# SwiGLU's first product: block sums and lower parts of the weights moved from VectorE to accumulating DMAs

## The chip, the cores and the metric

The kernel runs on one core of a Trainium2 chip. The metric is the device time of one execution in microseconds (us). Engines are named as in the profile: PE is TensorE, PEld its weight load, DVE VectorE, ACT ScalarE, POOL GpSimd, SP the queue from which the DMAs are issued in the kernel before.

## The reference

One layer of a streaming encoder in float32, 1024 tokens by 1024 channels: RMSNorm, one wide input projection for three mixers (convolution, gated linear attention, differential attention), gates, an output projection with residual, and then the channel mixing, where the change is:

```python
h = rms_norm(x, norm_ffn_g[l])
gate, up = jnp.split(h @ w_ffn_in[l], 2, axis=-1)
x = x + (jax.nn.silu(gate) * up) @ w_ffn_out[l]
```

`w_ffn_in` has 2 x 2816 columns, so that `h @ w_ffn_in` is a product of 1024 tokens by 1024 channels by 5632 columns.

## The kernel before

Every float32 product is made of three products of 1-pass operands: an operand is split into an upper part (`wh`, a rounded copy that ACT writes) and a lower part (`wl`, the operand less `wh`, which DVE writes), by `hilo` (L110 to L112), and `mm3` (L114 to L117) issues upper x upper, upper x lower and lower x upper. The loads are issued from SP.

The first product of SwiGLU goes over 22 units (`NU`) of 256 output columns, gate and up in turn. A unit's weights are 1 MB, four blocks of 128 x 512 (`a11`, `a21`, `a12`, `a22`; two halves of K by two halves of the columns). Each unit is taken by Winograd's form of Strassen's algorithm, in seven block products p = 0 to 6 in place of eight. Products 0, 3 and 5 have a plain block as left operand (`a11`, `a12`, `a22`); products 1, 2, 4 and 6 have sums of blocks: s1 = a21 + a22, s2 = s1 - a11, s3 = a11 - a21, s4 = a12 - s2, made on DVE by `comb` (L949 to L951). The right operands are blocks of h and their sums (`B`), made once ahead of the units in `ffn_norm`. A product is 4 steps of K by 3 matmuls of 512 columns, 12 matmuls.

The list `order` (L969 to L975) says in which order the products (unit, p) are taken, and `makes` in which order their operands are made. In the loop over `order`, `make()` runs seven products ahead (`AHEAD`, L62): it has the operand's sum made, then `operand()` (L133 to L137) splits it into one of eight pairs of buffers (`wh`, `wl`). The raw weights go into two buffers of half a unit (`wr`), the sums into four (`s2` with tag "s2", tiles named s1 to s4). The results are evicted behind the products: `copy` (ACT, L1006), `finish` (DVE adds, ACT silu for a gate unit; for an up unit DVE multiplies and SP stores to `m_d`, L991 to L1004). Each engine runs its instructions in the order in which they stand in its program, and a DMA that waits on SP or POOL holds up those that stand behind it there. That order is made by a recording layer, which moves instructions a little against the code, and semaphores do the rest.

Of the kernel before, what the change touches and what calls it, by code (L numbers as in the profile page):

```python
# [42 lines left out]
def units():  # L43
    """Order in which the 256-column weight units are consumed."""
    out = []
    for h in range(NH):
        out += [("CV", 2 * h), ("A", h), ("V", h), ("CV", 2 * h + 1), ("OG", h)]
        if h < NH - 1:
            out += [("MG", h)]
    for j in range(ND // 2):  # L50
        out += [("DV", j), ("QK", 2 * j), ("MD", j), ("QK", 2 * j + 1)]
    out += [("MG", NH - 1)] + [("MC", u) for u in range(4)]
    out += [("PW", u) for u in range(4)]
    out += [("WO", u) for _ in range(2) for u in range(4)]
    for j in range(FT // 2):
        out += [("FG", j), ("FU", j)]
    out += [("FO", j) for j in range(FT // 2)]
    return out
# [9 lines left out]
def body(nc, tc, I, out):  # L68
# [40 lines left out]

    def hilo(hi, lo, src):  # L110
        act.copy(hi, src)  # L111
        vec.tensor_tensor(out=lo, in0=src, in1=f(hi), op=ALU.subtract)  # L112

# [5 lines left out]
    def rstd(dst, ss, n, width):  # L119
        """dst = (ss / n + eps) ** -0.5"""  # L120
        vec.tensor_scalar(out=dst, in0=ss, scalar1=1.0 / n, scalar2=EPS, op0=ALU.mult, op1=ALU.add)
        pool.tensor_tensor(out=dst, in0=dst, in1=mhalf[:, 0:width], op=ALU.pow)  # L122

    # ---- weights: stream of units, one ahead of its use, split in pieces behind the products
    ready = deque()
# [48 lines left out]

    # ---- work that runs behind the projections: generators, each yields after how many
    # parts of a projection (8 products) it goes on
    events, clock = [], {"now": 0, "seq": 0, "conv": 0.0}
# [36 lines left out]

    # ---- hidden state, transposed: [channel, token] in two exact parts
    def transposed(src, hh, hl, half, gcol):
# [135 lines left out]

    # ================= A. convolution
    csum = q4("csum")[:, 0:S]
# [213 lines left out]

    # ================= C. differential attention
    A = {}  # L570
# [174 lines left out]

    # ================= convolution: LayerNorm over channels, swish
    def conv_norm(cs):
# [113 lines left out]
    def ffn_norm(t):  # L861
        xt = x2.pop(t)
        sp.dma_start(x2_d[t], xt)
        xn = b4("xn")
        ssc, rc = sm[:, 16 + t:17 + t], sm[:, 24 + t:25 + t]
        act.activation(xn, xt, AF.Square, accum_out=ssc)
        rstd(rc, ssc, D, 1)
        vec.scalar_tensor_tensor(out=xn, in0=xt, scalar=rc, in1=ffg, op0=ALU.mult, op1=ALU.mult)
        yield 4 if t in PARTS[0] else 3 if t < 4 else 2
        tt = slice(t % 4 * P, (t % 4 + 1) * P)  # L870
        v4 = lambda a: a.rearrange("p (k c) -> p k c", k=4)
        v4f = lambda a: a.bitcast(F32)

        def put(name, src):
            hilo(B[name][0][:, :, tt], B[name][1][:, :, tt], v4(src))

        pts = []
        for g in range(2):
            pt = bank()
            for k in range(4):  # L880
                pe.transpose(pt[:, k * P:(k + 1) * P], xn[:, (4 * g + k) * P:(4 * g + k + 1) * P], ident)
            pts.append(pt)
        old = lambda name, p: f(B[name][p][:, :, tt])
        if t < 4:
            put("11", pts[0])
            yield 2 if t in PARTS[0] else 0
            put("21", pts[1])
            return
        u, v = b4("u"), b4("v")
        t1, t2_, r12, t3 = u[:, hs(0)], u[:, hs(1)], v[:, hs(0)], v[:, hs(1)]  # L890
        vec.tensor_tensor(out=v4(t1), in0=v4(pts[0]), in1=old("11", 0), op=ALU.subtract)
        vec.tensor_tensor(out=v4(t1), in0=v4(t1), in1=old("11", 1), op=ALU.subtract)
        act.copy(r12, pts[0])
        put("T1", t1)
        yield 2 if t in PARTS[0] else 0
        vec.tensor_tensor(out=t2_, in0=pts[1], in1=t1, op=ALU.subtract)
        put("T2", t2_)
        yield 2 if t in PARTS[0] else 0
        put("22", pts[1])
        vec.tensor_tensor(out=t3, in0=pts[1], in1=r12, op=ALU.subtract)  # L900
        put("T3", t3)
# [25 lines left out]
    for half in range(2):  # L927
# [3 lines left out]
        for u in range(4):  # L931
            run(out_proj(half, u))
    # ================= SwiGLU, first product
    NU = FT
# [6 lines left out]
    def lefts(n):  # L941
        if n == 1:
            a11, a21, a12, a22 = (raw1[:, i, :] for i in range(4))
        else:
            r0 = raw_half(first + n, 0)
            r1 = raw_half(first + n, 1)
            a11, a21, a12, a22 = r0[:, 0:HALF], r0[:, HALF:], r1[:, 0:HALF], r1[:, HALF:]

        def comb(name, a, b, op):  # L949
            o = s2(name)  # L950
            vec.tensor_tensor(out=o, in0=a, in1=b, op=op)  # L951
            return o

        s_ = {}
        p = None
        while True:
            p = yield operand(s_[p]) if p is not None else None
            if p in (0, 3, 5):
                s_[p] = {0: a11, 3: a12, 5: a22}[p]
            elif p == 1:  # L960
                s_[1] = comb("s1", a21, a22, ALU.add)
            elif p == 2:
                s_[2] = comb("s2", s_[1], a11, ALU.subtract)
            elif p == 4:
                s_[4] = comb("s3", a11, a21, ALU.subtract)
            else:
                s_[6] = comb("s4", a12, s_[2], ALU.subtract)

    order = [(0, 0), (0, 3), (1, 0), (1, 3), (0, 1), (1, 1), (0, 2), (1, 2), (0, 4), (1, 4), (0, 6), (1, 6), (0, 5)]  # L969
    for n in range(1, NU):  # L970
        if n + 1 < NU:
            order.append((n + 1, 0))
        order += [(n, 5), (n, 6)] if n > 1 else [(n, 5)]
        if n + 1 < NU:
            order += [(n + 1, p) for p in range(1, 5)]  # L975
    makes = list(order)
# [5 lines left out]
    def make():  # L982
        if nxt[0] < len(makes):
            n, p = makes[nxt[0]]
            nxt[0] += 1
            if n not in gens:
                gens[n] = lefts(n)
                next(gens[n])
            made[n, p] = gens[n].send(p)

    def finish(n, i, k, add=None, src=None):  # L991
        gate = n % 2 == 0
        key = (n // 2, i, k)
        if add is not None:
            t = (y2 if len(fbs) == 0 else m2 if gate else c2)("t")
            vec.tensor_tensor(out=t, in0=src, in1=add, op=ALU.add)
            src = t
# [7 lines left out]

    def copy(src):  # L1006
        c = (c2 if fbs else y2)("c")
        act.copy(c, src)
        return c
# [12 lines left out]

    # the second product's operands
    mids, x3 = {}, {}
# [23 lines left out]
    for at, (n, p) in enumerate(order):  # L1048
# [35 lines left out]
        if p == 0:  # L1084
            ch["p1"] = copy(o)
        elif p == 2:
            ch["u2"] = copy(o)
        elif p == 3:
# [4 lines left out]
        elif p == 5:  # L1093
            finish(n, 1, 0, None, o)
        elif p == 6:
            finish(n, 0, 1, ch["u2"], o)

    drain()
    fbs[0].release()

    # ================= SwiGLU, second product, residual, RMSNorm
    fc = tc.alloc_tile_pool(name="fc", bufs=1)
# [107 lines left out]
```

## Time and profile before

| | |
|---|---|
| median of two runs | 2171.72 us (2170.72 to 2172.71) |
| span of the profiled execution | 2171.2 us, 0.5 us below the median |
| PE busy | 2147.5 us, 99% |
| DVE busy | 1385.6 us, 64% |
| ACT busy | 859.0 us, 40% |
| POOL busy | 45.5 us, 2% |
| SwiGLU's first product | from about 1497 to 1919 us of the span |

The table is read with the span: a busy share near 100% over the whole execution says that there is little room beside that engine, but the share of DVE or of ACT is a mean over stages, and what one stage waits for is read in that stage. PE's granted clock is a share of 2.4 GHz; 0.50 would be the lower of its two levels, 1.2 GHz.

### The profile page before, as it was taken

The numbers are of one execution on the slowest core, as the hardware profiler recorded it, in microseconds if no ns is written. First come the engines' busy times: TensorE is split into PE (matmuls) and PEld (weight loads), VectorE is DVE, ScalarE is ACT, GpSimd is POOL, SyncE is SP. The second block draws the span as 40 slices with busy tenths as digits, with TensorE's granted clock in tenths as the row PEclk, the third lists the DMA queues.
The fourth block names the chain that finished last, engine by engine and source line by source line (L and its number), as shares of the span: only waits on it lengthen the run. The fifth ranks groups of instructions, "written<-read, shape, count | busy, mean of one in ns | idle before, by whom it ended". The sixth has DMA issues, their size and how long they took to land.

```text
span 2171.2 us, 27863 instructions
## 1 busy us (share of the span) xinstructions
PE 2147.5 (99%) x10988; PEld 1787.7 (82%) x10988; DVE 1385.6 (64%) x2088; ACT 859.0 (40%) x1729; POOL 45.5 (2%) x45
## 2 busy tenths in 40 slices
PE   8999999999999999999999999999999999999998
PEld 6988988889887878778777888898888888888886
DVE  5988798789755454454545356567755545576766
ACT  6342251342345455455545354234433333341212
POOL 0000000000000000000000000000000000000000
PEclk9999999999999999999999999999999999999999
DMA  4112112121121111110111265443322222282111
GB/s 159 39 59 68 59 41 77 49 74 55 48 78 30 49 44 40 35 59 25 59 35 53 71 241 165 131 140 122 107 89 78 92 73 81 85 292 97 59 39 78
DMA packets 65059, 177.65 MB, mean 82 GB/s; under 512 B 6720, under 2 KB 17600, under 8 KB 64928
## 3 DMA queue, kind: packets, MB, share of 16 engines
q1 hardware_dynamic: 64928, 175.88, 24.4%
q8 instruction: 86, 1.41, 0.3%
q14 instruction: 45, 0.37, 0.1%
HBM read 137.58 MB, written 38.27 MB: 81 GB/s over the span
## 4 chain that ended last, share of the span: by engine, by line
PE 95%; DVE 3%; DMA 1%; issue 0%; POOL 0%; ACT 0%; SPq 0%; DVEq 0%; POOLq 0%; ACTq 0%
PE pb L115 22%; PE pb L116 22%; PE pb L117 22%; PE sc L115 6%; PE sc L116 5%; PE sc L117 5%; PE sc L643 3%; PE pb L678 3%; PE sc L642 3%; PE pb L667 1%; POOL sm L122 0%; DVE wl L112 0%; DVE xn L1127 0%; PE pb L712 0%; PE pb L504 0%
## 5 line engine op out<-in xcount | busy, mean ns | idle before, releaser
L115 PE MATMUL pb<-h,wh 128*128 128x512 f32 x1152 | 462.8, 402 | 0.0
L117 PE MATMUL pb<-h,wl 128*128 128x512 f32 x1152 | 450.9, 391 | 0.0
L116 PE MATMUL pb<-h,wh 128*128 128x512 f32 x1152 | 450.6, 391 | 0.0
L111 ACT CAST wh<-wr 128x512 fp32r<-128x512 f32 x331 | 203.5, 622 | 394.4 <-DVE x L1119 122.1
L112 DVE TENSOR_TENSOR wl<-wr,wh 128x512 fp32r<-128x512 f32 x331 | 225.5, 688 | 165.3 <-ACT wh L111 163.4
L362 DVE SCALAR_TENSOR_TENSOR acc<-up,par,acc 128x1024 f32<-128x1024 f32 x240 | 307.1, 1280 | 2.7
L115 PEld LDWEIGHTS pb<-h,wh 128*128 128x128 f32 x1152 | 217.1, 188 | 48.3 <-issue 5.1
L117 PEld LDWEIGHTS pb<-h,wl 128*128 128x128 f32 x1152 | 216.6, 188 | 46.8
L116 PEld LDWEIGHTS pb<-h,wh 128*128 128x128 f32 x1152 | 217.0, 188 | 41.3 <-DVE h L228 0.9
L1119 DVE TENSOR_TENSOR x<-x,pb 128x512 f32<-128x512 f32 x176 | 120.0, 684 | 59.8 <-PE pb L117 59.2
L115 PE MATMUL pb<-wh,h 128*128 128x256 f32 x512 | 148.1, 289 | 0.0
L117 PE MATMUL pb<-wh,h 128*128 128x256 f32 x512 | 144.9, 283 | 0.0
L116 PE MATMUL pb<-wl,h 128*128 128x256 f32 x512 | 144.8, 283 | 0.0
L115 PE MATMUL sc<-bT,wh 128*128 128x512 f32 x352 | 137.0, 390 | 0.5 <-ACT bT L111 0.5
L116 PE MATMUL pb<-wl,mh 128*128 128x512 f32 x352 | 136.9, 389 | 0.0
L115 PE MATMUL pb<-wh,mh 128*128 128x512 f32 x352 | 136.9, 389 | 0.0
L117 PE MATMUL pb<-wh,ml 128*128 128x512 f32 x352 | 136.9, 389 | 0.0
L116 PE MATMUL sc<-bT,wh 128*128 128x512 f32 x352 | 136.8, 389 | 0.0
L117 PE MATMUL sc<-bT,wl 128*128 128x512 f32 x352 | 136.6, 389 | 0.0
L111 ACT CAST wh<-s 128x512 fp32r<-128x512 f32 x88 | 54.5, 621 | 129.5 <-PE sc L116 79.4
L115 PEld LDWEIGHTS pb<-wh,h 128*128 128x128 f32 x512 | 98.1, 192 | 1.2 <-issue 0.6
L116 PEld LDWEIGHTS pb<-wl,h 128*128 128x128 f32 x512 | 98.1, 192 | 0.3
(249 smaller groups left out, 3768.2 us busy)
## 6 DMA issues: line engine op xcount, KB each, us to landing
wr<-w_dram SPq DMA_DIRECT2D x176, 512.0 KB, 3.6
m_d<-t SPq DMA_DIRECT2D x44, 256.0 KB, 2.1
mr<-m_d SPq DMA_DIRECT2D x22, 512.0 KB, 5.5
y_d<-y SPq DMA_DIRECT2D x28, 256.0 KB, 2.0
xt<-x_dram SPq DMA_DIRECT2D x8, 512.0 KB, 5.4
c_d<-acc SPq DMA_DIRECT2D x8, 512.0 KB, 2.7
g_d<-sgc SPq DMA_DIRECT2D x16, 256.0 KB, 2.1
c<-c_d SPq DMA_DIRECT2D x8, 512.0 KB, 7.8
```

The source lines that it names most:

```text
L111: act.copy(hi, src)
L112: vec.tensor_tensor(out=lo, in0=src, in1=f(hi), op=ALU.subtract)
L115: pe.matmul(o, ah, bh, start=start, stop=False, skip_group_check=more)
L116: pe.matmul(o, ah, bl, start=False, stop=False, skip_group_check=more)
L117: pe.matmul(o, al, bh, start=False, stop=stop, skip_group_check=more)
L362: vec.scalar_tensor_tensor(out=acc, in0=up[:, j:j + S], scalar=w, in1=acc, op0=ALU.mult, op1=ALU.add)
L642: pe.matmul(sc[i][:, c], a["q"][i][:, t], a["k"][i][:, c], start=True, stop=False)
L643: pe.matmul(sc[i][:, c], a["q"][i][L, t], a["kl"][L, c], start=False, stop=True)
L667: pe.transpose(pt[:, i * P:(i + 1) * P], pd[:, (g0 + i) * P:(g0 + i + 1) * P], ident)
L678: pe.matmul(ov[:, 0:P], parts[k // 4][:, c], a["v"][:, k, :], start=k == 0, stop=k == nk - 1)
L1119: vec.tensor_tensor(out=xx, in0=xx, in1=o, op=ALU.add)
```

## The change

Per unit, the sums are now made by DMA. Two buffers s1 and s3 are loaded with the block a21 (`begin`, a plain DMA from SP), and further blocks are added to them in place by DMAs from POOL that read HBM and add into the buffer (`plus`): s1 takes a22 (operand of product 1), then a11 (product 2), then a12 (product 6), and s3 takes a11 (product 4). The signs are arranged so that only additions occur: s1 for product 2 is a21 + a22 + a11, and the right operands "11" and "22" are stored with the opposite sign (`hilo` with `sign`, `put`, T1, T3), with matching signs in `copy` and `finish`. s1 is one buffer for three products, so a block is added only when the operand made from the earlier value has been read.

The lower part of each left operand is made so: ACT writes the negated operand into `wl` (`act.activation(wl, ..., scale=-1.0)`), whose buffer rounds as `wh` does, and a DMA from POOL adds the operand itself, from SBUF to SBUF. The order within a unit changes from p = 1, 2, 3, 4 to 1, 3, 2, 4 from the third unit on.

```diff
-        def comb(name, a, b, op):
+        def blk(i):
+            return w_d[first + n, i // 2, :, i % 2 * HALF:(i % 2 + 1) * HALF]
+        def begin(name):
             o = s2(name)
-            vec.tensor_tensor(out=o, in0=a, in1=b, op=op)
+            sp.dma_start(o, blk(1))
             return o
+        def plus(o, i):
+            pool.dma_start(o, blk(i), accum_op=ALU.add)
...
-            p = yield operand(s_[p]) if p is not None else None
-            if p in (0, 3, 5):
-                s_[p] = {0: a11, 3: a12, 5: a22}[p]
-            elif p == 1:
-                s_[1] = comb("s1", a21, a22, ALU.add)
-            elif p == 2:
-                s_[2] = comb("s2", s_[1], a11, ALU.subtract)
-            elif p == 4:
-                s_[4] = comb("s3", a11, a21, ALU.subtract)
-            else:
-                s_[6] = comb("s4", a12, s_[2], ALU.subtract)
+        s1, s3 = begin("s1"), begin("s3")
+        plus(s1, 3)
+        plus(s3, 0)
+        src = {0: a11, 3: a12, 5: a22, 1: s1, 2: s1, 6: s1, 4: s3}
+        def take(p):
+            wh = wp.tile([P, HALF], F32R, tag="wh", name="wh", bufs=8)
+            wl = wp.tile([P, HALF], F32R, tag="wl", name="wl", bufs=8)
+            act.copy(wh, src[p])
+            act.activation(wl, src[p], AF.Copy, scale=-1.0)
+            pool.dma_start(wl, src[p], accum_op=ALU.add)
+            o = wh, wl
+            if p in (1, 2):
+                plus(s1, (0, 2)[p - 1])
+            return o
...
-            order += [(n + 1, p) for p in range(1, 5)]
+            order += [(n + 1, p) for p in ((1, 3, 2, 4) if n > 1 else (1, 2, 3, 4))]
...
-            hilo(B[name][0][:, :, tt], B[name][1][:, :, tt], v4(src))
+            hilo(B[name][0][:, :, tt], B[name][1][:, :, tt], v4(src), -1.0 if name in ("11", "22") else 1.0)
...
-        act.copy(c, src)
+        act.activation(c, src, AF.Copy, scale=-1.0 if neg else 1.0)
```

On DVE, in the steady part of the units, stands before, for one unit (`s` are the sums, `wl` the lower parts, `t` the evictions):

```order
L951 TENSOR_TENSOR s1_13106<-wr_13047,wr_13049 128x512
L951 TENSOR_TENSOR s2_13126<-s1_13106,wr_13047 128x512
L951 TENSOR_TENSOR s3_13171<-wr_13047 128x512
L951 TENSOR_TENSOR s4_13234<-wr_13049,s2_13126 128x512
L996 TENSOR_TENSOR t_13085<-sc_12904,c_12981 128x512
L112 TENSOR_TENSOR wl_13109<-s1_13106,wh_13108 128x512
L112 TENSOR_TENSOR wl_13129<-s2_13126,wh_13128 128x512
L112 TENSOR_TENSOR wl_13150<-wr_13049,wh_13149 128x512
```

The sums and the lower parts are gone from DVE, where only the evictions (`t`) are left. POOL had no instruction in this stage; now its row for one unit is this, where L964 is `plus` (a block of the weights added from HBM) and L976 adds an operand into `wl`; s1_13079 and s3_13081 belong to one unit, s1_12944 to the unit ahead of it, s1_13231 and s3_13233 to the next:

```order
L964 DMA s1_13231<-w_dram 128x512
L976 DMA wl_13125<-s1_12944 128x512
L976 DMA wl_13142<-s1_13079 128x512
L976 DMA wl_13165<-wr_13077 128x512
L964 DMA s3_13233<-w_dram 128x512
L964 DMA s1_13079<-w_dram 128x512
L976 DMA wl_13184<-s1_13079 128x512
L976 DMA wl_13208<-s3_13081 128x512
L964 DMA s1_13079<-w_dram 128x512
L976 DMA wl_13238<-wr_13227 128x512
L976 DMA wl_13257<-wr_13077 128x512
```

So eleven accumulating DMAs per unit stand in one queue, and the addition to s3 of the next unit stands ahead of the second addition to s1 of this one. On SP stands now, for the same stretch (L960 is `begin`, L134 the raw halves, L1018 the store of an up unit):

```order
L960 DMA s1_13231<-w_dram 128x512
L134 DMA wr_13077<-w_dram 128x1024
L134 DMA wr_13227<-w_dram 128x1024
L960 DMA s3_13233<-w_dram 128x512
L1018 DMA m_d_86<-t_13029 128x512
L960 DMA s1_13382<-w_dram 128x512
```

Before, SP had only the raw halves and the stores there; the two loads of a21 per unit are new, and each needs one of the four sum buffers to be free.

## Rows read from the trace of the kernel before

**Rows 1.** The page: busy time, share of the span and instructions of each engine.

```profile
span 2171.2 us, 27863 instructions
PE 2147.5 (99%) x10988; PEld 1787.7 (82%) x10988; DVE 1385.6 (64%) x2088; ACT 859.0 (40%) x1729; POOL 45.5 (2%) x45
```

**Rows 2.** Busy time per window: window, its length, engines (instructions), PE clock, DMA share, GB/s.

```profile
1490.00:1495.00 5.00, 2.86 (x23) 2.34 (x22) 3.67 (x7) 4.14 (x9) 0.55 (x1) 1.00 0.91 363
1495.00:1500.00 5.00, 5.00 (x20) 3.93 (x19) 4.93 (x9) 1.85 (x4) 0.55 (x1) 0.66 0.13 52
1500.00:1900.00 400.00, 399.54 (x1749) 325.60 (x1748) 235.01 (x369) 153.95 (x267) 0.00 (x0) 1.00 0.26 86
```

**Rows 3.** What PE waited for between 1500 and 1900 us.

```profile
PE sc L115 <- ACT bT L111: 0.5, 1, 0.5
```

**Rows 4.** The chain that ended last, 1680 to 1860 us: start us, us, what.

```profile
1691.85 0.61 PE sc L115 x2
...
1730.38 0.61 PE sc L115 x2
...
1768.92 0.60 PE sc L115 x2
...
1807.42 0.61 PE sc L115 x2
...
1845.95 0.61 PE sc L115 x2
```

**Rows 5.** DVE and ACT by line and shape, 1500 to 1900 us.

```profile
L112 DVE TENSOR_TENSOR wl<-s,wh 128x512 fp32r<-128x512 f32 x87 | 59.2, 684 | 24.2 <-ACT wh L111 24.2
L112 DVE TENSOR_TENSOR wl<-wr,wh 128x512 fp32r<-128x512 f32 x61 | 42.1, 692 | 76.9 <-ACT wh L111 76.9
L951 DVE TENSOR_TENSOR s<-wr 128x512 f32<-128x512 f32 x41 | 28.2, 688 | 19.9 <-DMA wr<-w_dram 19.9
...
L111 ACT CAST wh<-s 128x512 fp32r<-128x512 f32 x86 | 53.3, 620 | 129.4 <-PE sc L116 79.4 <-DVE s L951 18.4 <-PE pb L116 14.6
...
L1008 ACT COPY c<-sc 128x512 f32<-128x512 f32 x63 | 36.6, 581 | 10.9 <-PE sc L117 10.9
```

**Rows 6.** DMA issues of the whole span: count, KB each, median us from issue to landing.

```profile
wr<-w_dram SPq DMA_DIRECT2D x176, 512.0 KB, 3.6
...
c<-c_d SPq DMA_DIRECT2D x8, 512.0 KB, 7.8
sg<-g_d SPq DMA_DIRECT2D x16, 256.0 KB, 3.3
...
x<-x_d SPq DMA_DIRECT2D x8, 512.0 KB, 5.5
```

**Rows 7.** DMA issues between 1495 and 1920 us.

```profile
m_d<-t SPq DMA_DIRECT2D x42, 256.0 KB, 2.0
```

**Rows 8.** SP's issuing of the stores to m_d: ns min/median/max, first and last start.

```profile
L1004 SPq DMA_DIRECT2D m_d<-t x44: 319/320/327, 1513.5 to 1927.2; - x44
```

**Rows 9.** POOL's instructions by line.

```profile
L122 POOL TENSOR_TENSOR rs<-rs,mhalf 128x8 f32<-128x8 f32 (+1 forms) x17 | 31.6, 1858 | 1225.6 <-DVE rs L121 1225.6
L122 POOL TENSOR_TENSOR sm<-sm,mhalf 128x1 f32<-128x1 f32 x24 | 13.7, 569 | 894.4 <-DVE sm L121 894.4
```

More of the change, by code (lines that the diff above doesn't have):

```diff
@@ L108, in f, with hilo @@
         return ap.bitcast(F32)
-    def hilo(hi, lo, src):
-        act.copy(hi, src)
-        vec.tensor_tensor(out=lo, in0=src, in1=f(hi), op=ALU.subtract)
+    def hilo(hi, lo, src, sign=1.0):
+        if sign > 0:
+            act.copy(hi, src)
+            vec.tensor_tensor(out=lo, in0=src, in1=f(hi), op=ALU.subtract)
+        else:
+            act.activation(hi, src, AF.Copy, scale=-1.0)
+            vec.scalar_tensor_tensor(out=lo, in0=src, scalar=-1.0, in1=f(hi), op0=ALU.mult, op1=ALU.subtract)
     def mm3(o, ah, al, bh, bl, start, stop, more=False):
@@ L890, in ffn_norm @@
         t1, t2_, r12, t3 = u[:, hs(0)], u[:, hs(1)], v[:, hs(0)], v[:, hs(1)]
-        vec.tensor_tensor(out=v4(t1), in0=v4(pts[0]), in1=old("11", 0), op=ALU.subtract)
-        vec.tensor_tensor(out=v4(t1), in0=v4(t1), in1=old("11", 1), op=ALU.subtract)
+        vec.tensor_tensor(out=v4(t1), in0=v4(pts[0]), in1=old("11", 0), op=ALU.add)
+        vec.tensor_tensor(out=v4(t1), in0=v4(t1), in1=old("11", 1), op=ALU.add)
         act.copy(r12, pts[0])
@@ L899, in ffn_norm @@
         put("22", pts[1])
-        vec.tensor_tensor(out=t3, in0=pts[1], in1=r12, op=ALU.subtract)
+        vec.tensor_tensor(out=t3, in0=r12, in1=pts[1], op=ALU.subtract)
         put("T3", t3)
@@ L947, in lefts @@
             a11, a21, a12, a22 = r0[:, 0:HALF], r0[:, HALF:], r1[:, 0:HALF], r1[:, HALF:]
-        def comb(name, a, b, op):
+        def blk(i):
+            return w_d[first + n, i // 2, :, i % 2 * HALF:(i % 2 + 1) * HALF]
+        def begin(name):
             o = s2(name)
-            vec.tensor_tensor(out=o, in0=a, in1=b, op=op)
+            sp.dma_start(o, blk(1))
             return o
-        s_ = {}
-        p = None
-        while True:
-            p = yield operand(s_[p]) if p is not None else None
-            if p in (0, 3, 5):
-                s_[p] = {0: a11, 3: a12, 5: a22}[p]
-            elif p == 1:
-                s_[1] = comb("s1", a21, a22, ALU.add)
-            elif p == 2:
-                s_[2] = comb("s2", s_[1], a11, ALU.subtract)
-            elif p == 4:
-                s_[4] = comb("s3", a11, a21, ALU.subtract)
-            else:
-                s_[6] = comb("s4", a12, s_[2], ALU.subtract)
+        def plus(o, i):
[14 more added lines that the diff above has]
+            return o
+        return take
     order = [(0, 0), (0, 3), (1, 0), (1, 3), (0, 1), (1, 1), (0, 2), (1, 2), (0, 4), (1, 4), (0, 6), (1, 6), (0, 5)]
@@ L987, in make, with finish @@
                 gens[n] = lefts(n)
-                next(gens[n])
-            made[n, p] = gens[n].send(p)
-    def finish(n, i, k, add=None, src=None):
+            made[n, p] = gens[n](p)
+    def finish(n, i, k, add=None, src=None, op=ALU.add):
         gate = n % 2 == 0
@@ L995, in finish @@
             t = (y2 if len(fbs) == 0 else m2 if gate else c2)("t")
-            vec.tensor_tensor(out=t, in0=src, in1=add, op=ALU.add)
+            vec.tensor_tensor(out=t, in0=add, in1=src, op=op)
             src = t
@@ L1004, in finish, with copy @@
             sp.dma_start(m_d[2 * (n // 2) + i, :, hs(k)], t)
-    def copy(src):
+    def copy(src, neg=False):
         c = (c2 if fbs else y2)("c")
-        act.copy(c, src)
+        act.activation(c, src, AF.Copy, scale=-1.0 if neg else 1.0)
         return c
@@ L1084, in body @@
         if p == 0:
-            ch["p1"] = copy(o)
+            ch["p1"] = copy(o, True)
         elif p == 2:
-            ch["u2"] = copy(o)
+            ch["u2"] = copy(o, True)
         elif p == 3:
@@ L1095, in body @@
         elif p == 6:
-            finish(n, 0, 1, ch["u2"], o)
+            finish(n, 0, 1, ch["u2"], o, ALU.subtract)
     drain()
```

## The prediction

> **What bounds the kernel now.** I read the page first: PE is busy for 2147.5 of 2171.2 us, and POOL does next to nothing [rows 1]. Then the stage that the change touches, in the table of windows: between 1500 and 1900 us PE is busy for 399.54 of 400 us at full granted clock, DVE for 235.01, ACT for 153.95, and the DMA engines are 0.26 busy at 86 GB/s [rows 2]. The list of waits says the same from the other side: in these 400 us PE waited once, for 0.5 us [rows 3]. So the stage runs at PE's own pace. That pace is read from the chain that ended last: the same pair of matmuls comes back at 1691.85, 1730.38, 1768.92, 1807.42 and 1845.95 us, every 38.53 us [rows 4]. A gate unit and an up unit lie between, so a unit takes 19.3 us, and 22 units some 424 us, which is the stage. Everything that the change does has to fit into 19.3 us per unit; what fits costs nothing, and what doesn't is paid for about 20 times.
>
> The same rows say what there is to win here: almost nothing. PE's only loss nearby is at the stage's start, 5.00 less 2.86 us busy between 1490 and 1495 us, after which the clock is 0.66 for 5 us [rows 2], 0.34 x 5 = 1.7 us lost: under 4 us together, and it comes from the norm and the output projection ahead, whose instructions stay.
>
> **What is taken away.** DVE loses, per unit, four sums and seven differences, eleven instructions of 684 to 692 ns [rows 5], 7.6 us of 19.3. None of it is on PE's path, since PE didn't wait for it. Saved: 0.
>
> **What ACT gets.** Seven negated copies more per unit, at the 620 ns of the copies beside them [rows 5]: 4.3 us. ACT was busy 153.95 of 400 us, 7.4 us per unit [rows 2]; it goes to 11.8 of 19.3. Hidden as throughput; in a chain each instruction counts (below). The signs in `hilo`, `copy` and `finish` replace one instruction by one of the same size and cost nothing.
>
> **What POOL, SP and the DMA engines get.** Per unit eleven accumulating DMAs of 256 KB from POOL and two plain loads of 256 KB from SP. As throughput: 86 GB/s by 19.3 us are 1.66 MB per unit now; 0.52 MB of plain loads and 2.88 MB of additions come on top, 5.1 MB, and 7.9 MB if the destination's re-reading counts as bytes. 86 GB/s at a share of 0.26 is 331 GB/s for all engines full, so they need 15.3 to 24.0 us per unit. That alone is close to 19.3.
>
> **The chain that the change builds.** The sums are no longer made from blocks that lie ready, but in steps that wait for each other through memory, and POOL's and SP's queues hold up what stands behind. With the names of the instruction lists of the change, followed from one unit to the next:
> 1. `wl_13125<-s1_12944` lands; only then is that sum's buffer free, and SP may load `s3_13233` into it: one plain load, P.
> 2. POOL has waited for that load before it issues the addition to `s3_13233`: one issue, g.
> 3. Behind it in POOL's queue stands the second addition to `s1_13079`: one accumulating DMA from issue to landing, A.
> 4. ACT then makes the operands of products 2 and 4 in its order, `wh`, an eviction, `wl`, `wh`, `wl`: five instructions of about 0.62 us [rows 5], 3.1 us.
> 5. POOL adds the operand into `wl_13208`: A. Its landing frees the buffer of `s3_13081`.
> 6. SP loads `s1_13382` into it: P. POOL waits for that and issues the addition to it: g.
> 7. Behind it stands `wl_13278<-s1_13079`: A. That is step 1 of the next unit.
>
> So a unit can't take less than 2 P + 3 A + 2 g + 3.1 us. The seven products that are made ahead (seven sevenths of a unit) shift this chain but don't shorten it.
>
> **The prices.** No row of the kernel before shows a DMA from POOL, or one that adds.
> - P: a load of 256 KB takes 3.3 us (`sg<-g_d`) [rows 6]; the ends are 2.0 us for a store of that size [rows 7] and 3.6 us for a load of twice the size [rows 6]. I take 3.3, the same size and direction.
> - g: SP's issue of such a DMA is 0.32 us [rows 8]; POOL's own instructions, tiny as they are, take 0.57 and 1.86 us [rows 9]. I take 1.0, between them, since POOL has to work it out in instructions.
> - A: at the least the 2.0 us of a plain transfer [rows 7] with SP's 0.32 for the issue, 2.3; at the most the 7.8 us of the slowest median [rows 6] with 1.86 for the issue, 9.7. An addition reads two operands, so I take a row of 512 KB; of those, 5.5 us (`x<-x_d`) [rows 6] is one that runs in this stage beside other transfers, and the engines will be busier than now. I let it include the issue. With the row 3.6 of `wr` [rows 6] and 1.0 for the issue A would be 4.6.
>
> The Trainium skill ("Collectives: The Full Stack", section "The bandwidth ceiling: the fold count and why AG ≠ RS ≠ AR") says that an adding transfer is slower not for its add but because it reads two sources, at about half the rate of a copy; no run here shows it yet. By that rule the rows of 512 KB are the right ones for A.
>
> **The sum.** 2 x 3.3 + 3 x 5.5 + 2 x 1.0 + 3.1 = 28.2 us per unit, 8.9 more than PE's 19.3. About 20 units are made in this steady order: 20 x 8.9 = 178 us, on 2171.2 us 2349, on the median 2350. With A = 4.6 a unit takes 25.5 us, 124 us more: 2296. With all upper ends, 2 x 3.6 + 3 x 9.7 + 2 x 1.86 + 3.1 = 43.1 us, 476 us more: 2648. With all lower ends, 4.0 + 6.9 + 0.6 + 3.1 = 14.6 us, less than 19.3: no change.
>
> **Rivals.**
> *Not slower: the chain closes within PE's pace.* With P = 3.3 and g = 1.0 this asks for 3 A below 19.3 - 6.6 - 2.0 - 3.1 = 7.6 us, A below 2.5; with the lower ends of P and g, for A below 3.9. Then PE never waits and the time is 2171, or up to 4 us less if the start is freed too. For it speaks that a store of 256 KB lands in 2.0 us. Against it, that loads take 3.3, that an addition does more, and that the engines' bytes alone may take 24.0 us. The Trainium skill ("DMA: Bandwidth & Descriptors", section "Anatomy of one DMA — SWDGE (gpsimd) path") fits a DMA from GpSimd by 2.0 us + bytes / 436e3 per us, which would be 2.6 us here; with it for P and A the estimate is 5.2 + 7.8 + 2.0 + 3.1 = 18.1 us and the time 2171. No row here bears on a DMA from GpSimd, so it counts only as a reason to keep this case.
> *The transfers are the bound, not their order.* If the DMA engines need 24.0 us per unit, the stage takes 20 x 4.7 = 94 us more: 2265. This is a floor under my forecast rather than another sign; it would show as a DMA share near 0.9 in the stage.
> *The additions are slow.* At A = 9.7 and the other upper ends, 2648. The rows reach 7.8 us only where transfers queue; that they do here is possible, as POOL may have several in flight.
> *PE's clock falls.* After 2.1 us without work the granted clock was 0.66 in the next 5 us [rows 2]. Waits of 9 us per unit would bring that again and again. PE isn't in the chain, so slow matmuls fill waiting time first; only if the whole stage ran at 1.2 GHz, 38.6 us per unit, would it be the bound: 20 x 19.3 = 386 us more, 2557.
>
> **How the numbers follow.** The chain with A between about 3.6 and 7 us, 2215 to 2500, carries 0.68, with the transfers' floor inside it; the chain closing, 0.12; the slow additions or the slow clock beyond 2500, 0.20, half of it below 2620. The likeliest is the sum, 2350. The range leaves out the case of no change and the far end: 2215 to 2620. A measurement of this kernel tells about 2%, 43 us, from no change: slower by more than that 0.87, within it 0.12. Faster by more has no mechanism in the rows, 0.01.
>
> **What would show it.** Right: in the stage PE idles some 9 us per unit and a pair of units takes near 56 us in place of 38.5; PE's matmuls wait for operands whose releaser is a DMA into `wl` or `s`; POOL's additions land after 4 to 7 us; DVE falls to the evictions; the time outside the stage is as before. Each price has its row there: the landing of the adding DMAs (A), POOL's time per issue (g), the loads of `s` (P). Wrong: additions that land in under 2.5 us with PE still at 399 of 400; or a DMA share near 1 in the stage, when order no longer matters; or POOL busy for the whole stage, when eleven issues of over 1.7 us are the bound.

## The result, and the profile after

The changed kernel takes 2435.99 us (median of two runs, 2433.64 to 2438.34) where the kernel before takes 2171.72: 1.1217 times as long, 95% interval 1.1196 to 1.1239, slower by 264 us. The forecast was 2350 with a range of 2215 to 2620.

The page of the kernel after, to set beside [rows 1]:

```profile
span 2436.6 us, 28353 instructions
PE 2196.4 (90%) x10988; PEld 1814.2 (74%) x10988; DVE 1235.4 (51%) x1846; ACT 933.6 (38%) x1883; POOL 257.7 (11%) x287
```

PE runs the same 10988 matmuls; 240 us of the span are now without one, against 24 before. Where they lie is told by the store to `m_d` and by a window of the stage. SP's stores to `m_d` after (ns min/median/max, first and last start), for [rows 8]:

```profile
L1018 SPq DMA_DIRECT2D m_d<-t x44: 319/383/1153, 1511.0 to 2192.7; - x44
```

The first store starts at 1511.0 us (1513.5 before), the last at 2192.7 (1927.2 before). So the stage is 268 us longer, and the rest of the program, within 3 us, as long as it was. The steady part of the stage in the kernel after (columns as in [rows 2]):

```profile
1600.00:2000.00 400.00, 268.66 (x1049) 210.97 (x1047) 43.43 (x63) 127.51 (x233) 117.42 (x134) 0.83 0.75 156
```

PE is busy for 268.66 of 400 us, DVE for 43.43, POOL for 117.42, and the DMA engines are 0.75 busy. A unit has 84 matmuls (seven products, four blocks, three passes), so 1049 are 12.5 units, 32.0 us each in place of 19.3. The unit times in the table of the experiments are worked out in this way. PE's waits in that window, for [rows 3]:

```profile
PE sc L119 <- ACT c L1022: 109.6, 10, 13.3
PE sc L119 <- DVE t L1010: 17.9, 2, 9.0
```

PE waits about once per unit, some 11 us each, and for ACT's copy of an accumulated bank, not for an operand. The timelines of one unit show what ACT waits for in its turn. Those of PE, of ACT, of SP and of POOL, 1812 to 1847 us (start us, us, instruction, idle time before it and what ended it):

```profile
1813.26 0.79 PE L119 MATMUL sc<-bT,wh 128*128 128x512 f32 x1 [10.30 <-ACT c L1022]
...
1846.68 0.80 PE L119 MATMUL sc<-bT,wh 128*128 128x512 f32 x1 [11.02 <-ACT c L1022]
```

```profile
1812.09 0.62 ACT L974 CAST wh<-s 128x512 fp32r<-128x512 f32 x1 [12.51 <-DMA s<-w_dram]
1812.62 0.59 ACT L1022 ACTIVATE c<-sc 128x512 f32<-128x512 f32 x1
...
1823.52 0.62 ACT L974 CAST wh<-s 128x512 fp32r<-128x512 f32 x1 [1.32 <-PE sc L120]
...
1845.52 0.62 ACT L974 CAST wh<-s 128x512 fp32r<-128x512 f32 x1 [12.26 <-DMA s<-w_dram]
```

```profile
1819.06 0.33 SPq L960 DMA_DIRECT2D s<-w_dram  x1
...
1824.64 0.33 SPq L134 DMA_DIRECT2D wr<-w_dram  x1
...
1826.10 0.33 SPq L134 DMA_DIRECT2D wr<-w_dram  x1
1833.66 0.33 SPq L960 DMA_DIRECT2D s<-w_dram  x1
```

```profile
1814.13 0.86 POOL L976 DMA_DIRECT2D wl<-s  x1 [6.70 <-ACT wl L975]
1815.17 0.86 POOL L976 DMA_DIRECT2D wl<-s  x1 [0.18 <-issue]
1818.10 0.89 POOL L964 DMA_DIRECT2D s<-w_dram  x1 [2.07 <-DMA wl<-s]
...
1823.34 1.03 POOL L964 DMA_DIRECT2D s<-w_dram  x1
1825.08 0.88 POOL L976 DMA_DIRECT2D wl<-s  x1 [0.72 <-ACT wl L975]
...
1837.55 0.87 POOL L964 DMA_DIRECT2D s<-w_dram  x1 [7.75 <-DMA s<-w_dram]
...
1838.72 1.49 POOL L964 DMA_DIRECT2D s<-w_dram  x1
```

Read from the first ACT row to the last, this is the ring of the forecast. ACT starts the cast for product 2 at 1812.09. POOL starts product 4's addition at 1815.17 (3.1). It lands, and SP loads `s` at 1819.06 (A, 3.9). POOL adds to that load at 1823.34 (P, 4.3), and starts the sum's last operand at 1825.08 (g, 1.7). It lands, and SP loads the next sum at 1833.66 (A, 8.6). POOL adds to that at 1837.55 (P, 3.9), and starts the addition behind it at 1838.72 (g, 1.2). It lands at 1845.52 (A, 6.8), and ACT casts product 2 of the next unit. That is 33.4 us, of which A has 19.3, P 8.2, g 2.9 and ACT 3.1. In the twelve units from 1618 to 2006 us the cast for product 2 comes back every 32.3 us on average, and the landing that took 8.6 us here takes 7.6 to 9.1 us in each. The eviction `c`, for which PE waits, stands in ACT's queue behind that cast. (The chain that ended last reaches back only into the stage's last units, so it has no rows beside [rows 4].)

The prices have rows of their own: POOL's issues by line in the 400 us (g: 0.90 to 1.0 us), and the DMA issues there, for [rows 6, 7]:

```profile
L964 POOL DMA_DIRECT2D s<-w_dram x48 | 46.3, 1005 | 122.8 <-DMA s<-w_dram 99.0 <-DMA wl<-s 17.7 <-PE sc L121 5.7
L976 POOL DMA_DIRECT2D wl<-s x49 | 43.6, 902 | 116.3 <-ACT wl L975 113.9 <-issue 2.2
```

```profile
q0 software_dynamic: 19567, 35.63, 54.1%
...
wl<-s POOLq DMA_DIRECT2D x49, 256.0 KB, 5.4
s<-w_dram POOLq DMA_DIRECT2D x48, 256.0 KB, 4.5
wl<-wr POOLq DMA_DIRECT2D x37, 256.0 KB, 4.4
s<-w_dram SPq DMA_DIRECT2D x25, 256.0 KB, 3.6
```

The plain loads take 3.6 us (P), the additions 4.4 to 5.4 (A) by their medians. ACT's negated copies take what was assumed (ACT by line in the 400 us, for [rows 5]):

```profile
L975 ACT ACTIVATE wl<-s 128x512 fp32r<-128x512 f32 x49 | 30.6, 624 | 0.0
L974 ACT CAST wh<-s 128x512 fp32r<-128x512 f32 x49 | 30.2, 616 | 200.2 <-DMA s<-w_dram 156.4 <-PE sc L120 38.0 <-PE sc L121 3.0
```

### The profile page after: what moved, and what is told of

It reads as the page before. It is cut to its first block, busy times and chain, and to the rows that moved or that the text cites. A ratio compares the mean times of both kernels' runs of the same rounds, so it can differ in the third digit from the quotient of the medians.

```text
span 2436.6 us, 28353 instructions
## 1 busy us (share of the span) xinstructions
PE 2196.4 (90%) x10988; PEld 1814.2 (74%) x10988; DVE 1235.4 (51%) x1846; ACT 933.6 (38%) x1883; POOL 257.7 (11%) x287
## 3 DMA queue, kind: packets, MB, share of 16 engines
q1 hardware_dynamic: 71264, 187.41, 23.2%
## 5 line engine op out<-in xcount | busy, mean ns | idle before, releaser
L119 PE MATMUL sc<-bT,wh 128*128 128x512 f32 x352 | 160.6, 456 | 197.2 <-ACT c L1022 164.9
L112 ACT CAST wh<-wr 128x512 fp32r<-128x512 f32 x268 | 164.2, 622 | 305.1 <-DVE x L1133 139.3
L1010 DVE TENSOR_TENSOR t<-c,sc 128x512 f32<-128x512 f32 x44 | 30.2, 687 | 448.1 <-ACT c L1022 349.0
L119 PEld LDWEIGHTS sc<-bT,wh 128*128 128x128 f32 x352 | 76.7, 218 | 227.7 <-ACT c L1022 173.4
L113 DVE TENSOR_TENSOR wl<-wr,wh 128x512 fp32r<-128x512 f32 x268 | 182.1, 688 | 85.3 <-ACT wh L112 84.2
L126 POOL TENSOR_TENSOR rs<-rs,mhalf 128x8 f32<-128x8 f32 (+1 forms) x17 | 31.6, 1859 | 1224.0 <-DVE rs L125 1176.5
L121 PE MATMUL sc<-bT,wl 128*128 128x512 f32 x352 | 152.3, 433 | 3.9 <-DMA wl<-s 3.9
L120 PE MATMUL sc<-bT,wh 128*128 128x512 f32 x352 | 153.8, 437 | 0.0
```

What stands on the lines that cost most here:

```text
L119: pe.matmul(o, ah, bh, start=start, stop=False, skip_group_check=more)
L120: pe.matmul(o, ah, bl, start=False, stop=False, skip_group_check=more)
L121: pe.matmul(o, al, bh, start=False, stop=stop, skip_group_check=more)
L1010: vec.tensor_tensor(out=t, in0=add, in1=src, op=op)
```

## The experiments

The theory: steps that wait for each other through memory set 32 us per unit. Its rivals: the engines' bytes or the number of additions; POOL's issues; PE's clock; PE's wait for the eviction alone. Each time is a median of two to four runs, beside the kernel before on the same chip (medians 2170.35 to 2171.72).

| run | us | against before | 95% | unit, us |
|---|---|---|---|---|
| after | 2435.99 | 1.1217 | 1.1196 to 1.1239 | 32.0 |
| e1_lower_only | 2198.65 | 1.0118 | 1.0101 to 1.0135 | 20.2 |
| e2_sums_only | 2246.62 | 1.0344 | 1.0329 to 1.036 | 23.2 |
| e3_eight_buffers | 2436.46 | 1.1217 | 1.1195 to 1.1239 | 31.6 |
| e4_no_add | 2316.98 | 1.0667 | 1.0646 to 1.0688 | 26.5 |
| e5_half | 2348.61 | 1.0821 | 1.0775 to 1.0868 | 27.7 |
| e7_no_raw | 2384.84 | 1.0988 | 1.0941 to 1.1036 | 29.0 |
| e8_first_on_dve | 2357.94 | 1.0864 | 1.0818 to 1.0911 | 28.3 |
| e9_later_on_dve | 2290.29 | 1.0553 | 1.0507 to 1.0598 | 25.3 |
| e11_sums_lower_dve | 2286.43 | 1.0532 | 1.0465 to 1.0598 | 24.6 |
| e12_plain_lower_dve | 2368.68 | 1.091 | 1.0879 to 1.0942 | 28.9 |
| e10_warm | 2478.23 | 1.1415 | 1.1369 to 1.1461 | 34.4 |
| e13_evict_dve | 2428.81 | 1.1198 | 1.1175 to 1.122 | 30.9 |

The last column is from the matmuls between 1600 and 2000 us (to 1900 us in e1 and e2, whose stage ends sooner); in e10 a unit has 116. The ends of the window cut units, so it is good to about 1 us: e3 has the time of the kernel after and shows 31.6 for its 32.0.

**One part at a time.** The kernel before with the lower parts alone made by POOL:

```diff
+        def lower(src):
...
+            act.copy(wh, src)
+            act.activation(wl, src, AF.Copy, scale=-1.0)
+            pool.dma_start(wl, src, accum_op=ALU.add)
...
-            p = yield operand(s_[p]) if p is not None else None
+            p = yield lower(s_[p]) if p is not None else None
```

> Half of the change: the sums of blocks are made on VectorE as in the kernel before, and only the lower parts come from an accumulating DMA (7 of 11 per unit). Chain theory (the loss is one ring of waits through memory that needs both halves, 31.2 us per unit against 19.3): without the sums' DMAs the lower parts are made seven products ahead and nobody waits for them one after the other, so the stage returns to PE's pace: 2171 to 2195 us. Rival, each accumulating DMA costs PE a share wherever it is: 7/11 of the 264 us, 2340. Rival, ScalarE's extra negated copies hold up the evictions: 2200 to 2250.

And the kernel after with the sums alone made by POOL, the lower parts again by DVE:

```diff
-            act.copy(wh, src[p])
-            act.activation(wl, src[p], AF.Copy, scale=-1.0)
-            pool.dma_start(wl, src[p], accum_op=ALU.add)
+            hilo(wh, wl, src[p])
```

> The other half: the sums come from accumulating DMAs (4 per unit), the lower parts from VectorE as before. Chain theory: the three landings of additions in the ring become at most one, and VectorE's 0.69 us stands in place of the others: two loads of 3.6, one addition of 4.7, two issues of 0.95, five instructions of 0.65 make 17 us, under 19.3: 2171 to 2200 us. Rival, a share for each accumulating DMA: 4/11 of 264, 2267. Rival, the serial additions to one buffer are slow by themselves: over 2300.

27 us and 75 us, 102 together, against 264 for both. The first is only just outside what was expected (2198.65 for at most 2195), and 1 us under the rival that has ACT's copies hold up the evictions; since PE's waits from 1600 to 2000 us are nearly all for ACT's eviction (8.6 us, 15 times), that rival isn't excluded for these 27 us. The second is 47 us above its expectation. Of the forecast's ring 2 P, 2 g, one A and ACT's part are left, 7.6 + 1.8 + 4.7 + 3.1 = 17.2 us by this run's prices (P 3.8, A 4.7, g 0.9), under PE's 19.3, and a unit takes 23.2. One unit of this run in the timelines of ACT, PE, SP and POOL, 1812 to 1836 us, shows another loop:

```profile
1812.51 1.14 ACT L112 CAST wh<-s 128x512 fp32r<-128x512 f32 x2 [5.26 <-DMA s<-w_dram]
...
1821.99 0.62 ACT L112 CAST wh<-s 128x512 fp32r<-128x512 f32 x1 [2.17 <-PE sc L120]
...
1835.42 0.62 ACT L112 CAST wh<-s 128x512 fp32r<-128x512 f32 x1 [7.24 <-DMA s<-w_dram]
```

```profile
1814.19 0.50 PE L119 MATMUL sc<-bT,wh 128*128 128x512 f32 x1 [1.30 <-ACT c L1020]
```

```profile
1823.49 0.33 SPq L960 DMA_DIRECT2D s<-w_dram  x1
```

```profile
1828.88 1.75 POOL L964 DMA_DIRECT2D s<-w_dram  x2 [9.35 <-DMA s<-w_dram]
```

The eviction for which PE waits stands behind ACT's casts for products 2 and 4 (1812.51), and PE starts at 1814.19. ACT's next cast of a sum, product 6's at 1821.99, waits for PE, which has to be done with an operand pair first. DVE's difference then frees the sum's buffer, SP loads into it at 1823.49, and POOL adds to that load at 1828.88, with the addition to `s1` behind it, which lands for the next product 2 at 1835.42, 22.9 us after the first cast. So 9.5 us of this loop go through PE and the operand pairs, a stretch that the forecast's sum doesn't hold. Seven additions per unit without the sums cost a tenth of what the eleven cost: it is not their number. Either part alone leaves links out of the ring and stays nearer to PE's pace; with both it takes all of them, and what is over 19.3 us is paid in full.

**More buffers.** The second kind of sum gets four buffers of its own:

```diff
-            o = s2(name)
+            if name == "s3" and fbs:
+                o = fbs[0].tile([P, HALF], F32, tag="s3", name=name, bufs=4)
+            else:
+                o = s2(name)
```

> The whole change with eight sum buffers in place of four (s3 of the later units in four of its own). Chain theory as in the prediction (the ring runs through the release of a sum buffer and the load into it): the loads start early, two loads of 3.6 us and one landing drop out, what is left is a ring of four landings of some 4.5 us and their copies per unit, about 22 to 25 us with the transfers less bunched: 2235 to 2300 us. Rival, the ring through s1 alone (add, copy, lower part, add again, in one queue) is as long as the one through the buffers: no gain, 2400 to 2440. Rival, the transfer engines (0.75 busy now, 23.4 us of 31.2 per unit): 2255, with their share near 1.

No change, which is the rival's number. SP's largest wait in the 400 us of this run:

```profile
SPq L963 <- DMA wl<-s: 296.3, 25, 17.7
```

The load goes on waiting for an addition: in the program's order it stands right behind the release of the buffer that it takes, whichever that is, and POOL's in-order queue takes the steps in the same order (POOL waited 97.1 us of the 400 for loads of `s`, 99.0 in the kernel after). That more buffers alone don't break the ring is shown. Whether the rival's ring through s1 would be as long isn't, and a version in which the first additions stand later in POOL's queue wasn't run.

**The price of an addition.** First the same transfers as plain copies:

```diff
-            pool.dma_start(o, blk(i), accum_op=ALU.add)
+            pool.dma_start(o, blk(i))
...
-            pool.dma_start(wl, src[p], accum_op=ALU.add)
+            pool.dma_start(wl, src[p])
```

> The whole change, but the DMAs from GpSimd copy and don't add (the sums and the lower parts are left out; the output is not the reference's). If adding makes a transfer slow by its second read, a copy lands about 1 us sooner alone and more where transfers are bunched, three landings per ring: 27 to 28 us per unit, 2350 to 2370. Rival, a DMA from GpSimd is as slow without the addition: unchanged, 2425 to 2440. The busy share of the transfer engines tells the same apart: 55.1% for the queue in the stage now, 27 to 35% if the read counts twice.

The kernel leaves out the sums and the lower parts. 2316.98, 119 us less, more than expected. The transfers of the run (software queue, then issues, 1600 to 2000 us), and POOL's issue:

```profile
q0 software_dynamic: 19921, 43.26, 34.6%
...
s<-w_dram POOLq DMA_DIRECT2D x60, 256.0 KB, 3.3
wl<-s POOLq DMA_DIRECT2D x60, 256.0 KB, 2.7
```

```profile
L976 POOL DMA_DIRECT2D wl<-s x60 | 32.0, 533 | 149.9 <-ACT wl L975 149.8
```

A falls to 2.7 to 3.3 us by the medians and g from 0.9 to 0.53. With those the sum would be 2 x 3.1 + 3 x 3.0 + 2 x 0.53 + 3.1 = 19.4 us, PE's pace, and the unit takes 26.5. The ring, read in the timelines as above, tells why. One of its steps there, in POOL's and in SP's rows:

```profile
1815.22 0.53 POOL L976 DMA_DIRECT2D wl<-s  x1 [1.54 <-ACT wl L975]
```

```profile
1813.29 0.33 SPq L134 DMA_DIRECT2D wr<-w_dram  x1
...
1815.06 0.33 SPq L134 DMA_DIRECT2D wr<-w_dram  x1
...
1821.24 0.33 SPq L960 DMA_DIRECT2D s<-w_dram  x1
```

This copy lands after 6.0 us, twice the median, with two loads of `wr` beside it. The ring's three landings are 2.3, 6.0 and 4.1 us, P is 4.3 and 3.8, g 2.1 and 1.2, ACT 3.1: 26.9 us. So the ring closes with copies too. The adding itself is worth 7 of A's 19.3 us. Of the 7.5 us over the sum the landings have 3.4, 3.0 of them in that one copy: a step in which the transfers of one turn meet is not priced by a median. P and g have the other 4.1; at the first of both POOL waited for ACT's operands (the row at 1815.22), not for the load.

Then additions over half the columns:

```diff
-            pool.dma_start(o, blk(i), accum_op=ALU.add)
+            pool.dma_start(o[:, 0:256], blk(i)[:, 0:256], accum_op=ALU.add)
...
-            pool.dma_start(wl, src[p], accum_op=ALU.add)
+            pool.dma_start(wl[:, 0:256], src[p][:, 0:256], accum_op=ALU.add)
```

> The change with each accumulating DMA cut to half its columns (the other half of the sums and of the lower parts is left out; the output is not the reference's). If the landing is mostly a fixed time, a landing alone falls from 3.3 to about 2.8 us and the bunched ones more: 26 to 28 us per unit, 2320 to 2360 us. If the landing is bytes at the transfer engines' rate, all landings halve, and the ring falls under 22 us: 2230 or less.

2348.61, as the theory had it, from a kernel that leaves half of every addition out. Half the bytes land in 3.1 to 3.4 us where all of them take 4.4 to 5.4, by the medians about a third less and not half; a bound by the bytes would have given 2230 or less.

Then the kernel leaves out the loads of the raw blocks, which run beside the additions, from the fifth unit on:

```diff
+    halves = []
...
-            r0 = raw_half(first + n, 0)
-            r1 = raw_half(first + n, 1)
+            if n < 4:
+                halves[:] = [raw_half(first + n, 0), raw_half(first + n, 1)]
+            r0, r1 = halves
```

> The change without the loads of the raw halves from the fifth unit on (the plain operands stay those of the fourth; the output is not the reference's). It tells what the bunching of transfers costs: a lower part that was issued just ahead of two loads of 512 KB landed after 8.50 us in place of 3.3 to 3.8. Chain theory: 4 us less for that landing and about 1 for others, 18 units: 2340 to 2370 us. Rival, the transfers don't disturb each other in the ring: 2425 to 2440.

51 us less, between the two expectations. In the ring of this run (1806 to 1830 us) the three landings are 5.0, 6.0 and 3.9 us, 14.9 in place of 19.3: the loads of `wr` lengthen A, and two of the three landings stay above 3.9 us without them.

**Links of the ring, one at a time.** The first additions of both sums go to DVE, from the blocks that lie ready:

```diff
-        s1, s3 = begin("s1"), begin("s3")
-        plus(s1, 3)
-        plus(s3, 0)
...
+            if p == 1:
+                src[1] = src[2] = src[6] = s2("s1")
+                vec.tensor_tensor(out=src[1], in0=a21, in1=a22, op=ALU.add)
+            elif p == 4:
+                src[4] = s2("s3")
+                vec.tensor_tensor(out=src[4], in0=a11, in1=a21, op=ALU.add)
```

> The change with the first sums (s1 = a21 + a22, and s3) made on VectorE, so that no load of a21 and no first addition is left; the two later additions into s1 and the lower parts stay accumulating DMAs (9 per unit). Theory of the prediction (one ring through the release of a buffer, the load into it and the first addition in GpSimd's queue): both loads and both issues are gone and the ring with them, 2171 to 2210 us. Rival, a second ring of about the same length through s1 itself, lower part landed, addition landed, copies, lower part landed, addition landed, and ScalarE's queue behind it: four landings of about 4.5 us and 5 us of copies, 23 us: 2240 to 2300 us.

2357.94, 78 us less than after, but 148 us above what the theory of one ring expected and above its rival too. The loads and their additions (2 P and 2 g of the sum) are gone, and another wait stands in their place, SP's for the buffers of the raw blocks:

```profile
SPq L134 <- DMA wl<-wr: 219.6, 19, 22.5
```

In the unit from 1712.08 to 1739.43 us of its timelines the steps follow each other so: product 1's lower part lands in 4.5 us, the addition to `s1` in 4.3, product 2's lower part in 3.7 and, behind the next addition in POOL's queue, a plain block's lower part in 4.5; that frees a raw buffer, whose load and sum take 5.2 us to the next unit's product 1. That is a second loop, through `s1` and the raw buffers, 27.4 us long.

The later additions to `s1` go to DVE, and the new sums into buffers of their own:

```diff
+            if p in (2, 6):
+                new = fbs[0].tile([P, HALF], F32, tag="s3", name="s2", bufs=4) if n > 1 else s1
+                vec.tensor_tensor(out=new, in0=src[1 if p == 2 else 2], in1=a11 if p == 2 else a12, op=ALU.add)
+                src[p] = new
...
-            if p in (1, 2):
-                plus(s1, (0, 2)[p - 1])
```

> The other way round: the first sums by load and accumulating DMA, the two later ones on VectorE into buffers of their own, the lower parts by accumulating DMA (9 per unit). Theory of the prediction: the ring loses one landing and the copies' wait for it: two loads of 3.6, two landings of 4.7, two issues of 0.95, copies of 3: 21.6 us per unit, 2200 to 2240 us. Rival, the second ring through s1 alone is the cause: it is gone, 2171 to 2200 us. Rival, GpSimd's queue held up by the loads is the whole of it: 2350 or more.

2290.29, 146 us less for two additions of eleven (the buffers of their own brought nothing by themselves in e3), though short of the 2200 to 2240 expected: what is left, 25.3 us per unit, is again a wait for transfers (DVE's for `wr` 209.8 us of the 400, SP's for `wl` 178.0 and 150.5).

**Number against place.** The lower parts of the four sums go to DVE, and in a second kernel those of the three plain blocks:

```diff
-            act.copy(wh, src[p])
-            act.activation(wl, src[p], AF.Copy, scale=-1.0)
-            pool.dma_start(wl, src[p], accum_op=ALU.add)
+            if p in (1, 2, 4, 6):   # the second kernel: (0, 3, 5)
+                hilo(wh, wl, src[p])
+            else:
+                act.copy(wh, src[p])
+                act.activation(wl, src[p], AF.Copy, scale=-1.0)
+                pool.dma_start(wl, src[p], accum_op=ALU.add)
```

> The whole change, but the lower parts of the four sums of a unit are made on VectorE as before; those of the three plain blocks stay accumulating DMAs (7 of 11 left). Chain theory: the lower parts of the sums are links of the rings, each a landing of 4 to 8 us, and are replaced by 0.7 us; close to the run with the sums alone (2247): 2230 to 2290 us. Rival, the loss goes with the number of accumulating DMAs: 2171 + 264 x 7/11 = 2339.

> The counterpart: the lower parts of the three plain blocks on VectorE, those of the four sums stay accumulating DMAs (8 of 11 left). Chain theory: all links of the ring through the sums are still there, only less bunched: 27 to 30 us per unit, 2340 to 2400 us, a small part of the loss although three DMAs are gone. Rival, by number: 2171 + 264 x 8/11 = 2363, so this run tells only together with the other: by the chain theory the two lie some 100 us apart, by number 24.

2286.43 and 2368.68, both as expected. One has four additions fewer and the other three; by their number they would stand 24 us apart, and they stand 82 apart. The additions that count most are those whose landing frees a sum's buffer or gives the next addition its turn. That the plain blocks' three still bring 67 us may come from the transfers that they no longer put beside the others (the medians of the rest fall from 5.4 and 4.5 us to 3.9 and 4.1); it wasn't separated.

**PE's own part.** To hold PE's clock up, 32 matmuls into a spare bank stand ahead of product 2:

```diff
+        if p == 2 and 2 < n < NU - 1:
+            warm = bank()
+            for _ in range(32):
+                pe.matmul(warm, B["11"][0][:, 0, 0:P], B["T1"][0][:, 0, :], start=True, stop=True)
```

> The whole change with 32 extra matmuls of 512 columns per unit on TensorE, into a spare bank that nobody reads, just ahead of the product of s2, where TensorE waits for some 11 us per unit (extra work of 7.3 us at full clock, or 14.5 at half). It raises the granted clock in the stage from 0.83. If the slower clock is no part of the ring, the time stays at 2425 to 2450 us; if the evictions on a slow TensorE hold up ScalarE's queue in the ring, it falls to 2380 to 2415.

Neither: 42 us slower than after. The window of the run, 1600 to 2000 us, and POOL's timeline at the place where product 2's and product 4's additions are issued:

```profile
1600.00:2000.00 400.00, 334.77 (x1348) 266.84 (x1347) 40.27 (x59) 118.80 (x217) 111.06 (x126) 0.90 0.70 146
```

```profile
1685.30 0.86 POOL L976 DMA_DIRECT2D wl<-s  x1 [6.14 <-ACT wl L975]
1688.99 0.88 POOL L964 DMA_DIRECT2D s<-w_dram  x1 [2.83 <-DMA wl<-s]
1689.64 1.13 POOL L976 DMA_DIRECT2D wl<-s  x1
```

The mean clock rises from 0.83 to 0.90, but the edit did something that wasn't meant: in POOL's queue the addition to `s1`, which waits for product 2's landing, now stands ahead of product 4's addition, where in the kernel after it stands behind it (1814.13, 1815.17, 1818.10). Product 4's is issued 4.3 us after product 2's in place of 1.0. That puts 3.3 us more into the ring, and the unit grew by 2.4. So the run leaves open what the clock is worth, since the order changed with it. The growth fits the swap in POOL's queue, but the 32 matmuls came with it, so that the swap alone costs this much isn't shown.

Last, the evictions go from ACT to DVE, so that PE's bank no longer waits behind ACT's cast:

```diff
-        act.activation(c, src, AF.Copy, scale=-1.0 if neg else 1.0)
+        vec.tensor_scalar(out=c, in0=src, scalar1=-1.0 if neg else 1.0, scalar2=None, op0=ALU.mult)
```

> The whole change with the eviction copies (three per unit) on VectorE, which idles, in place of ScalarE. In the profile of the change TensorE stands still because the copy that empties its bank stands in ScalarE's queue behind a cast that waits for an addition to s1; TensorE then starts at half clock, and ScalarE's next cast waits 6 us for the pair of buffers that its first product frees. If this path through TensorE is what makes the ring longer than the landings alone, it drops out: 28 to 29 us per unit, 2350 to 2400 us, and a higher clock. Rival, the path through the load of a21 and the first addition is just as long (in the unit from 1812 us it was ready at 1824.4, the other at 1824.7): 2415 to 2440 us although TensorE idles less in one piece. Nearer to 2171 than 2300 would say that the landings don't matter at all.

2428.81, as the rival had it: 7 us less, and the slowest of its runs (2436.44) lies among those of the kernel after. PE's largest wait in this run, and ACT's timeline over one unit:

```profile
PE sc L119 <- ACT t L1014: 113.8, 6, 19.3
```

```profile
1806.78 0.62 ACT L974 CAST wh<-s 128x512 fp32r<-128x512 f32 x1 [11.84 <-PE sc L120]
...
1839.61 0.62 ACT L974 CAST wh<-s 128x512 fp32r<-128x512 f32 x1 [12.55 <-DMA s<-w_dram]
```

PE waits as long as before, for another instruction of ACT, and the ring closes in 32.8 us by the same steps, with landings of 3.9, 9.1 and 6.3 us. The eviction that PE waited for is where the ring reaches PE, not what makes it long.

## Why the prediction was right

**Where and what.** What DVE lost brought nothing, and the time outside the stage is unchanged, as predicted. The stage turned from PE's pace to a ring of waits, once per unit, and its steps stand in the timelines one by one in the order that was written down. That steps which wait for each other through memory cost the time, rather than the number of instructions, is shown by e9 and e11 (a few links taken out, 146 and 150 us back), by e12 against e11, and by e13, where PE's wait was moved and the time stayed; e10 fits it. That there is only this one ring, as the experiments' theory had it, is not so: behind it stand a loop through `s1` and the raw buffers (27.4 us in the unit of e8) and one through PE and the operand pairs (22.9 us in the unit of e2), and a change that shortens the ring runs into them.

**The terms.** P was taken as 3.3 and is 3.6 by its median, 3.9 and 4.3 in the ring. g was taken as 1.0 and is 0.90 to 1.0. ACT's 3.1 is 3.1. The term that was mis-sized is A: taken as 5.5 with its issue, it measures 3.9, 8.6 and 6.8 in the ring read above, 19.3 us for the three in place of 16.5. The row of 512 KB had the right size for its median, 4.4 to 5.4 from issue to landing, and missed what a unit's own transfers do to it: the addition of 8.6 us was issued between two loads of `wr` at 1824.64 and 1826.10, while the DMA engines were at 0.99 in the ten microseconds that follow 1820:

```profile
1820.00:1830.00 10.00, 10.00 (x45) 7.99 (x44) 2.99 (x5) 3.98 (x8) 4.38 (x5) 1.00 0.99 209
```

With P at 8.2, A at 19.3, g at 2.9 and 3.1 for ACT the sum is 33.5 us, and 20 units would give 284 us; it was 264, which the mean of 32.3 us fits (20 x 13.0 = 260). The working of the range has a slip: by the sum, A of 3.6 to 7 us gives 2235 to 2440, and not the 2215 to 2500 set against it.

**"PE isn't in the chain"** was wrong, at a price of about a microsecond here. The forecast looked for PE waiting on DMAs into `wl` or `s`; it waits for ACT's eviction, which stands behind the cast. After that wait PE starts at half clock (its first 5 us, the granted clock third from the end):

```profile
1813.20:1818.20 5.00, 4.94 (x12) 3.88 (x13) 0.00 (x0) 1.56 (x4) 1.83 (x3) 0.50 0.55 95
```

ACT's casts behind it then wait for the operand buffers that PE frees, and POOL's first two additions to `wr` operands with them, ahead of the ring's step at 1823.34; so does product 6's cast at 1823.52, whose addition follows at 1825.08. So two arms lead from product 2's cast to that addition, the forecast's over product 4's landing and the load, and one over PE, and in this unit the second ended last. That may be why P is 4.3 there and 3.9 at its other place, and g 1.7 and 1.2: 0.9 us per unit by that comparison. The forecast took the products made ahead for a mere shift of the chain; that the arm through PE, 13.0 us here, is no longer than the one it had summed up is luck, and e2, which shortened that one, met it. What the clock alone costs wasn't separated.

**The rivals.** *Not slower* fell with A: it needed 2.5 to 3.9 us. The Trainium skill ("DMA: Bandwidth & Descriptors", section "Anatomy of one DMA — SWDGE (gpsimd) path") has a fit that gives an estimate of 2.6 us for this size; the copies of e4 land in 2.7 to 3.3, near it, the additions of the kernel after in 4.4 to 5.4. *The transfers are the bound* had its upper number right, 0.75 of 32.0 us being 24.0 us of all engines per unit, but that is a floor under the ring and not the bound; it enters through A. *The additions are slow* overstated A. *PE's clock falls* is there, 0.83 in the stage, but PE is busy for 21.5 of the unit's 32.0 us, so it isn't the bound by itself; its matmuls at half clock stand in the arm through PE.

## What to carry to other kernels

When work that lay side by side is turned into steps that wait for each other through memory, cost the loop of waits that returns to the same buffer, queue by queue, and compare it with the bound engine's time per turn; the share of busy time of the queues (POOL 0.29, DMA 0.75 here) shows no danger. Take the price of a transfer in such a loop from the transfers that the same turn issues beside it, not from a median alone. Follow every arm of the loop, also the one that is no longer than the others: it holds up the next change. When a loop is too long, take its link that frees a buffer out of memory (here two additions of eleven were worth 146 us) before adding buffers, which left the time as it was; and look where each addition stands in its in-order queue.

## What the runs showed of the hardware that was not expected

- An addition by DMA holds the engines about twice as long as a copy. In the kernel after the software queue has 54.1% of 400 us for 134 transfers of 256 KB, 1.6 us each over all engines; in e4 34.6% for 166 copies, 0.83 us. The Trainium skill ("Collectives: The Full Stack", section "The bandwidth ceiling: the fold count and why AG ≠ RS ≠ AR") says of the adding transfers of a ReduceScatter that they read two sources and run at about half the rate of copies; these rows agree.
- POOL's issue costs 0.90 to 1.0 us for an addition and 0.53 for a copy, and half the bytes hardly make it shorter, 0.87 for 0.90 at the same line (POOL by line in e5):

```profile
L976 POOL DMA_DIRECT2D wl<-s x58 | 50.4, 869 | 130.0 <-ACT wl L975 130.0
```

- The landing of additions of one size, 256 KB from SBUF to SBUF, spreads by a factor of three (the whole span of the kernel after, line 976):

```profile
DMA to landing us min/median/max: 3.3/4.7/10.1
```
